# S5's gate inputs in places of their own, head norms summed by column quarters, meta products as whole tiles

## The chip, the core and the metric

One core of a Trainium2 chip runs the whole kernel. TensorE (PE) multiplies, VectorE (DVE) and ScalarE (ACT) work on tiles in the on-chip memory SBUF and read products out of PSUM, GpSimd (POOL) does a few side jobs, SyncE (SP) issues the loads. All engines run beside each other; each works its own queue in order and waits on semaphores. The metric is the device time of one execution in microseconds (us), as a median over runs.

## The reference

One layer of a hybrid encoder over 16 meta tokens and 256 tokens, width 2048, all in float32.

```python
xn = rmsnorm(h, norm_mix); q, f, i, g, u = split(xn @ w_in)      # 5 x 1024 columns
# HGRN2, 8 heads of 128: chunkwise gated recurrence
f = lb + (1 - lb) * sigmoid(f); k = (1 - lb) * sigmoid(-f_logit); q = silu(q)
S_t = diag(f_t) S_{t-1} + k_t v_t^T;  o_t = S_t^T q_t
o = o * rsqrt(mean(o * o over the head) + EPS) * gain * silu(g)   # head norm
# S5, 64 groups of 16 channels, complex diagonal state of 64
y = Re(C x_t) + d * u;  y = gelu(y)
y = y * sigmoid(y @ w_glu + b_glu);  y = rmsnorm(y)               # the gate (GLU)
h = h + concat(o, y) @ w_out
h = h + conv_ffn(rmsnorm(h))                                      # 2048 -> 2 x 5632 -> 2048
out = rmsnorm(h[16:])
```

## The kernel before

Everything is kept channel-major: 128 channels on the partitions, tokens along the columns (272 with the meta tokens, 258 where only the last two of them are needed). Each large product is made as three matmuls in a fast float32 form: weights are split into a high part `whi` (ACT, L163) and the rest `wlo` (DVE, L85), activations likewise into `xh`/`xl`, `gh`/`gl`, `mh`/`ml`; `mm3` (L187 to L189) runs high x high, low x high, high x low into a PSUM tile `acc`. Weights come in 1 MB pieces; `whi` and `wlo` have three buffers each, a piece takes two, and three `acc` tiles rotate.

The mixer runs in the order `u0 h0 u1 h1 u2 h2 u3 h3 g0 .. g3`. A `u` chunk feeds two S5 tiles: projection `bu` (L602, 64-row matmuls), a scan on DVE with ACT and POOL (ending in `xo`, the state), the output products `yps` (L616 and L621, 32-column matmuls), and then the GELU in five steps on DVE and ACT: `ysb` (scale and add), `gq` squared (ACT), `gq` (DVE), sigmoid (ACT), `ysb` (product). An `h` chunk pair makes two HGRN2 heads: the scores `dps`, `lps`, `xps`; then the meta tokens' part, `mps` = `km` x `qm` (L761, 16 meta tokens as 16 output columns), copied to `sm`, and the output `ops`, whose first matmul `vm` x `sm` (L766) contracts over those 16 rows; three more (L767 to L769) follow. `oT` holds the heads' outputs, `gs` the output gates.

Behind the mixer: `gh`/`gl` are made from all eight `ysb` tiles, in one tile of the pool `tl`, which is opened where the pool of S5's working tiles (`s5w`) is closed, in the same memory. The GLU's four products with `w_glu` read them (`acc<-gh`); each result gates `ysb` (`sgl`) and its square is added into `ssum`, summed over channels by `s5s` (L847). The head norm: `sq` squares a head, `hps` (L857) sums it over channels into row h of an 8-row PSUM tile by a weight matrix of 8 columns; `rsqrt` makes the scale in some 13 steps on DVE (`rhv`, `rht`, `rhy`); `hr2` keeps it as high part and rest in 40 rows; `bps` (L868) spreads one head's row over 128 partitions by a 40-row matmul, one at a time in PSUM; then `oT` is scaled and split into `mh`/`ml`. `w_out` is applied in two halves, the first over the HGRN2 heads, the second over S5. The gated MLP follows.

The order on each engine is not that of the code: a scheduler lays the instructions out by a simulated timeline, within priorities (`pri`) and the dependencies of the tiles, and a tile's place in memory makes dependencies too. So an edit of a few lines moves rows all over the mixer stage.

Of the kernel before, what the change touches and what calls it, by code (L numbers as in the profile page):

```python
# [73 lines left out]
def hymba_kernel(ctx: ExitStack, tc: tile.TileContext, x, meta, lb_logits, norm_mix, w_in, hg_norm,  # L74
# [9 lines left out]
    def tt(dst, a, b, op, eng=dve):  # L84
        eng.tensor_tensor(out=dst, in0=a, in1=b, op=op)  # L85
# [572 lines left out]
    def hg_i(accs):  # L658
        iv = hgp.tile([128, 2, T], F32, tag="iv", name="iv")
        for m in range(2):  # L660
            act.copy(out=iv[:, m], in_=accs[m])
# [4 lines left out]
        v = hgp.tile([128, 4, 128], F32, tag="v", name="v")
        act.copy(out=v, in_=tp)
        tp = ptp.tile([128, 4, 128], F32, tag="tp", name="vtp")
        for m in range(2):
            pe.transpose(tp[0:NM, m], iv[:, m, 0:NM], ident)  # L670
        vm = hgp.tile([NM, 2, 128], F32, tag="vm", name="vm")
        act.copy(out=vm, in_=tp[0:NM, 0:2])
        return v, vm

    def hg_g(h0, accs):
        sg = hgp.tile([128, 2, NQ], F32, tag="sg", name="sg")
# [1 line left out]
            fact(sg[:, m], accs[m], AF.Sigmoid)  # L678
            stt(gs[:, h0 + m], accs[m], vcol[:, V_HG + h0 + m:V_HG + h0 + m + 1], sg[:, m], MUL, MUL)

    def hg_group(h0, f, k, q, v, vm):
        SP = hgp.tile([128, 2, T], F32, tag="SP", name="SP")
        pool.memset(SP, 1.0)

# [53 lines left out]
            widen(h)  # L738
        return S, SP

    def hg_cross(h0, f, f15, k, q, v, vm, S, SP):
        kx = hgp.tile([128, 2, 128], F32, tag="qh", name="kx", bufs=3)
        tt(kx, k[:, :, NM:NM + 128], SP[:, :, NM:NM + 128], MUL)
        km = hgp.tile([128, 2, NM], F32, tag="km", name="km")
        tt(km, k[:, :, 0:NM], SP[:, :, 0:NM], MUL)
# [12 lines left out]
        sm = hgp.tile([NM, 2, NQ], F32, tag="iv", name="sm")  # L758
        for m in range(2):
            ps = psc.tile([128, NQ], F32, tag="sc", name="mps")  # L760
            pe.matmul(ps[0:NM], km[:, m], qm[:, m], start=True, stop=True)  # L761
            act.copy(out=sm[:, m, 1:NQ], in_=ps[0:NM, 1:NQ])
            ts(sm[:, m, 0:1], ps[0:NM, 0:1], misc[0:NM, 17:18], MUL)
        for m in range(2):
            ps = psc.tile([128, NQ], F32, tag="sc", name="ops")
            pe.matmul(ps, vm[:, m], sm[:, m], start=True, stop=False)  # L766
# [1 line left out]
            pe.matmul(ps[:, 130:NQ], v[:, 2 * m], sx[:, m], start=False, stop=False)
            pe.matmul(ps[:, 130:NQ], v[:, 2 * m + 1], S[:, 2 * m + 1], start=False, stop=True)  # L769
# [45 lines left out]
    tlp = tls.enter_context(tc.tile_pool(name="tl", bufs=1))  # L815


    gh = tlp.tile([128, 8, 2 * NQ], F32R, name="gh")
    gl = gh[:, :, NQ:2 * NQ]
    gh = gh[:, :, 0:NQ]  # L820

    def sp_view(a):
        return a.rearrange("p (s k) -> p s k", s=2)

    for j in range(8):
        yv = ysb[:, j, :, K0:TH]
        act.copy(out=sp_view(gh[:, j]), in_=yv)
# [22 lines left out]
    mh = xnp.tile([128, KD, T], F32R, tag="xh", name="mh")  # L850
    ml = xnp.tile([128, KD, T], F32R, tag="xl", name="ml")
    with pri(-2):
        hps = psc.tile([8, NQ], F32, tag="sc", name="hps")
        for h in range(NH):
            sq = hgp.tile([128, NQ], F32, tag="qh", name="sq", bufs=3)
            fact(sq, oT[:, h], AF.Square)
            pe.matmul(hps, onehot[:, 7 - h:15 - h], sq, start=(h == 0), stop=(h == NH - 1))  # L857
# [4 lines left out]
        tt(hr2[32:40], hrs, hr2[0:8].bitcast(F32), SUB)
        hsel = hgp.tile([40, NH], F32R, tag="f15", name="hsel")
        dve.tensor_copy(out=hsel, in_=misc[0:40, 18:26])
        for h in range(NH):
# [2 lines left out]
            pe.matmul(bp, hsel[:, h:h + 1].to_broadcast([40, 128]), hr2, start=True, stop=True)  # L868
# [192 lines left out]
```

## Time and profile before

| | us |
|---|---|
| median of 3 runs | 1241.25 (1241.08 to 1242.11) |
| the profiled execution | 1245.4, of which span 1243.6 |
| PE busy | 1220.0 |
| DVE busy | 878.6 |
| ACT busy | 605.9 |
| mean granted PE clock | 0.991 |

The span runs from the first to the last instruction. In rows of the order of time, the first number is the start in us from the span's beginning, the second the length; "x2" merges records of one kind, and an fp32 matmul leaves two records. Ends of matmuls are modelled and they overlap, so what a matmul costs is read from start to start. In brackets stands the idle time of the engine ahead of the row and who ended it.

### The profile page before, as it was taken

To read this page: it belongs to the slowest core of one execution; us is meant where nothing else is said; L and a number is where in the kernel's file an instruction comes from. 1 tells how busy PE (TensorE), PEld (TensorE's weight loads), DVE (VectorE), ACT (ScalarE), POOL (GpSimd) and SP (SyncE) were. 2 spreads that over 40 slices of the span, in tenths; PEclk is the share of its full clock that TensorE was granted. 3 is DMA by queue.
4 is the path that set the end of the run, shared out by engine and by line. 5 is a ranking of instruction groups with operands and counts; after the bars stand their busy time and mean duration, and the time that the engine had idled before them with its cause. 6 is when DMAs were issued, how large, how long until landed. Compare 5 with 4: busy or idle time off the path is not lost.

```text
span 1243.6 us, 22643 instructions
## 1 busy us (share of the span) xinstructions
PE 1220.0 (98%) x9235; PEld 1146.4 (92%) x9235; DVE 878.6 (71%) x1535; ACT 605.9 (49%) x1054; POOL 91.1 (7%) x116
## 2 busy tenths in 40 slices
PE   7999999999999999999999999999999999999997
PEld 6999998989979999999999999999999988888886
DVE  7899999999977877765656656656656644545554
ACT  6756566675645455433433433434333434444454
POOL 5221211322100000000000000000000000000000
PEclk8999999999999999999999999999999999999999
DMA  8454443334335555565555656555565645555552
GB/s 241 147 149 131 143 142 106 113 109 144 127 102 169 171 178 196 170 195 179 183 190 176 197 171 194 179 184 190 174 199 170 230 165 184 200 201 184 191 208 97
DMA packets 176295, 210.73 MB, mean 169 GB/s; under 512 B 14772, under 2 KB 168879, under 8 KB 170415
## 3 DMA queue, kind: packets, MB, share of 16 engines
q1 hardware_dynamic: 175871, 209.20, 51.8%
q8 instruction: 72, 1.18, 0.4%
q14 instruction: 32, 0.26, 0.1%
q0 software_dynamic: 320, 0.09, 0.0%
HBM read 206.05 MB, written 2.10 MB: 167 GB/s over the span
## 4 chain that ended last, share of the span: by engine, by line
PE 95%; DVE 3%; DMA 1%; issue 0%; ACT 0%; SPq 0%; DVEq 0%; ACTq 0%
PE acc L189 10%; PE acc L188 10%; PE acc L187 9%; PE ua L188 7%; PE ua L187 7%; PE ga L187 7%; PE ua L189 7%; PE ga L189 7%; PE ga L188 7%; PE d L984 6%; PE d L982 6%; PE d L983 6%; PE bu L602 1%; PE lps L731 1%; DVE wlo L85 1%; DVE xn L94 1%
## 5 line engine op out<-in xcount | busy, mean ns | idle before, releaser
L85 DVE TENSOR_TENSOR wlo<-raw,whi 128x1024 fp32r<-128x1024 f32 (+1 forms) x376 | 461.2, 1227 | 305.1 <-ACT whi L163 255.6
L163 ACT CAST whi<-raw 128x1024 fp32r<-128x1024 f32 (+1 forms) x382 | 397.8, 1042 | 517.2 <-PE ga L188 158.2
L187 PE MATMUL ga<-fh,whi 128*128 128x258 f32 x704 | 199.0, 283 | 0.5 <-DVE a L85 0.5
L189 PE MATMUL ga<-fh,wlo 128*128 128x258 f32 x704 | 198.5, 282 | 0.0
L188 PE MATMUL ua<-fl,whi 128*128 128x256 f32 x704 | 198.4, 282 | 0.0
L188 PE MATMUL ga<-fl,whi 128*128 128x258 f32 x704 | 198.1, 281 | 0.0
L189 PE MATMUL ua<-fh,wlo 128*128 128x256 f32 x704 | 197.9, 281 | 0.0
L187 PE MATMUL ua<-fh,whi 128*128 128x256 f32 x704 | 197.9, 281 | 0.0
L188 PE MATMUL acc<-xl,whi 128*128 128x272 f32 (+1 forms) x640 | 186.9, 293 | 2.3 <-DVE xl L85 2.3
L189 PE MATMUL acc<-xh,wlo 128*128 128x272 f32 (+1 forms) x640 | 184.3, 293 | 3.8 <-DVE wlo L85 3.8
L187 PE MATMUL acc<-xh,whi 128*128 128x272 f32 (+1 forms) x640 | 185.9, 294 | 0.0
L187 PEld LDWEIGHTS ga<-fh,whi 128*128 128x128 f32 x704 | 133.0, 189 | 0.7 <-DVE a L85 0.7
L188 PEld LDWEIGHTS ga<-fl,whi 128*128 128x128 f32 x704 | 133.5, 190 | 0.0
L187 PEld LDWEIGHTS ua<-fh,whi 128*128 128x128 f32 x704 | 133.1, 189 | 0.0
L189 PEld LDWEIGHTS ua<-fh,wlo 128*128 128x128 f32 x704 | 132.9, 189 | 0.0
L188 PEld LDWEIGHTS ua<-fl,whi 128*128 128x128 f32 x704 | 132.8, 189 | 0.0
L189 PEld LDWEIGHTS ga<-fh,wlo 128*128 128x128 f32 x704 | 132.6, 188 | 0.0
L982 PE MATMUL d<-whi,ah 128*128 128x512 f32 x328 | 127.7, 389 | 0.0
L188 PEld LDWEIGHTS acc<-xl,whi 128*128 128x128 f32 x640 | 121.8, 190 | 6.4 <-DVE xl L85 3.2
L983 PE MATMUL d<-whi,al 128*128 128x512 f32 x328 | 127.6, 389 | 0.0
L189 PEld LDWEIGHTS acc<-xh,wlo 128*128 128x128 f32 x640 | 120.9, 191 | 6.7 <-DVE wlo L85 4.3
L187 PEld LDWEIGHTS acc<-xh,whi 128*128 128x128 f32 x640 | 121.1, 190 | 3.3 <-issue 1.7
(381 smaller groups left out, 1840.3 us busy)
## 6 DMA issues: line engine op xcount, KB each, us to landing
raw<-in_w_ffn_gate SPq DMA_DIRECT2D x44, 1024.0 KB, 5.1
raw<-in_w_ffn_up SPq DMA_DIRECT2D x44, 1024.0 KB, 5.1
raw<-in_w_ffn_down SPq DMA_DIRECT2D x44, 1024.0 KB, 4.8
raw<-in_w_in SPq DMA_DIRECT2D x39, 1024.0 KB, 5.2
raw<-in_w_out SPq DMA_DIRECT2D x16, 1024.0 KB, 5.4
raw<-in_w_glu SPq DMA_DIRECT2D x4, 1024.0 KB, 5.2
x<-in_x SPq DMA_DIRECT2D x4, 512.0 KB, 5.9
out<-ob SPq DMA_DIRECT2D x8, 256.0 KB, 2.8
```

Of the source, the lines that this page charges most:

```text
L85: eng.tensor_tensor(out=dst, in0=a, in1=b, op=op)
L94: dve.scalar_tensor_tensor(out=dst, in0=a, scalar=s, in1=b, op0=op0, op1=op1, **kw)
L163: act.copy(out=hi[:, c], in_=raw[:, hf, c])
L187: pe.matmul(accs[m], lh, xh[:, n0:n1], start=first, stop=False)
L188: pe.matmul(accs[m], lh, xl[:, n0:n1], start=False, stop=False)
L189: pe.matmul(accs[m], ll, xh[:, n0:n1], start=False, stop=end)
L602: return pe.matmul(bus[i][:, ri], bt[h, 2 * ri + q0 // 2], R[h, q0 // 2], start=True, stop=True)
L731: pe.matmul(ps[:, i], kt[:, i], qf[:, 64 * i:64 * (i + 1)], start=True, stop=True)
L982: pe.matmul(dps[t][n], ah[:, tk], hi, start=False, stop=False, skip_group_check=True)
L983: pe.matmul(dps[t][n], al[:, tk], hi, start=False, stop=False, skip_group_check=True)
L984: pe.matmul(dps[t][n], ah[:, tk], lo, start=False, stop=end, skip_group_check=True)
```

## The change

- `gh`/`gl` get one tile for each of the eight S5 tiles: three in the S5 pool, which is open from the start, three in places of the HGRN2 pool that held `f`, `k` and `q` (tags `PP`, `k`, `q`), two in `tl`.
- `km` and `vm` become whole tiles of 128 columns or rows, cleared once by POOL; `mps` gives 128 rows, of which 112 are zero, and `ops` contracts over 128 rows.
- A head's sum goes into one of four 32-column quarters of a 128-row PSUM tile: heads 2q and 2q+1 into quarter q, on alternate rows. The sums are issued in the order 0, 2, 4, 6, 1, 3, 5, 7. The scale is made on all 128 rows; rows 0 and 1 of a quarter keep the high part, rows 2 and 3 the rest (two DVE steps with column masks, `ht` and `hr`), and `bps` contracts over 128 rows, with two PSUM buffers (`bu`) instead of one.
- The constants `misc` grow from 26 to 69 columns.

```diff
-    misc = np.zeros((128, 26), np.float32)
+    misc = np.zeros((128, 69), np.float32)
...
-    misc[:, 18:26] = (s[:, None] % 32 == np.arange(NH)) & (s[:, None] < 64)
+    misc[:, 18:26] = (s[:, None] // 32 == hd // 2) & (s[:, None] % 2 == hd % 2) & (s[:, None] % 32 < 4)
+    misc[:, 26] = (s % 32 < 2) * 1.0 - ((s % 32 >= 2) & (s % 32 < 4))
+    misc[:, 27] = (s % 32 >= 2) & (s % 32 < 4)
+    misc[:, [29, 31]] = 1.0
...
     ysb = s5p.tile([128, 8, 2, TH], F32, name="ysb")
+    ghs = [s5p.tile([128, 2 * NQ], F32R, name=f"gh{i}") for i in range(3)]
...
+    km = hgp.tile([128, 2, 128], F32, name="km")
+    vm = hgp.tile([128, 2, 128], F32, name="vm")
+    for k in kts + [S, km, vm]:
         pool.memset(k, 0.0)
...
-        vm = hgp.tile([NM, 2, 128], F32, tag="vm", name="vm")
-        act.copy(out=vm, in_=tp[0:NM, 0:2])
+        act.copy(out=vm[0:NM], in_=tp[0:NM, 0:2])
...
-        sm = hgp.tile([NM, 2, NQ], F32, tag="iv", name="sm")
+        sm = hgp.tile([128, 2, NQ], F32, tag="iv", name="sm")
         for m in range(2):
             ps = psc.tile([128, NQ], F32, tag="sc", name="mps")
-            pe.matmul(ps[0:NM], km[:, m], qm[:, m], start=True, stop=True)
+            pe.matmul(ps, km[:, m], qm[:, m], start=True, stop=True)
...
-    gh = tlp.tile([128, 8, 2 * NQ], F32R, name="gh")
+    ghs += [hgp.tile([128, 2 * NQ], F32R, tag=t, name="gh" + t) for t in ("PP", "k", "q")]
+    ghs += [tlp.tile([128, 2 * NQ], F32R, name=f"gh{i}") for i in (6, 7)]
+    gh, gl = [z[:, 0:NQ] for z in ghs], [z[:, NQ:2 * NQ] for z in ghs]
...
-        hps = psc.tile([8, NQ], F32, tag="sc", name="hps")
-        for h in range(NH):
+        hps = psc.tile([128, NQ], F32, tag="sc", name="hps")
+        for h in (0, 2, 4, 6, 1, 3, 5, 7):
             sq = hgp.tile([128, NQ], F32, tag="qh", name="sq", bufs=3)
             fact(sq, oT[:, h], AF.Square)
-            pe.matmul(hps, onehot[:, 7 - h:15 - h], sq, start=(h == 0), stop=(h == NH - 1))
-        hrs = rsqrt(hgp, hps, [8, NQ], 1.0 / 128, "rh", tags=("iv", "qm", "v"))
-        hr2 = hgp.tile([40, NQ], F32R, tag="SP", name="hr2")
-        pool.memset(hr2.bitcast(F32), 0.0)
-        act.copy(out=hr2[0:8], in_=hrs)
-        tt(hr2[32:40], hrs, hr2[0:8].bitcast(F32), SUB)
+            pr = slice(16 * h - 16 * (h % 2), 16 * h - 16 * (h % 2) + 32)
+            pe.matmul(hps[pr], misc[:, 29 - h % 2:61 - h % 2], sq, start=(h % 2 == 0), stop=(h % 2 == 1),
+                      skip_group_check=True)
+        hrs = rsqrt(hgp, hps, [128, NQ], 1.0 / 128, "rh", tags=("iv", "qm", "v"))
+        hr = hgp.tile([128, NQ], F32R, tag="SP", name="hr")
+        ht = hgp.tile([128, NQ], F32, tag="iv", name="ht")
+        act.copy(out=hr, in_=hrs)
+        ts(ht, hr.bitcast(F32), misc[:, 26:27], MUL)
+        stt(hr, hrs, misc[:, 27:28], ht, MUL, ADD)
...
-            bp = psc.tile([128, NQ], F32, tag="sc", name="bps")
-            pe.matmul(bp, hsel[:, h:h + 1].to_broadcast([40, 128]), hr2, start=True, stop=True)
+            bp = pbu.tile([128, NQ], F32, tag="bu", name="bps")
+            pe.matmul(bp, hsel[:, h:h + 1].to_broadcast([128, 128]), hr, start=True, stop=True)
```

What the scheduler makes of it is seen at the two places below. Line numbers of the new code are higher: `mm3` is L191 to L193 there, `yps` L621 and L626, `bps` L879.

PE around the start of the GLU, before. The last S5 tile's output products (`yps`) stand among the head sums, then 33 plain matmuls of the last `g` chunk, then the GLU:

```order
L616 MATMUL yps<-xo,cp_570 32x136 x6
L621 MATMUL yps<-xo,cp_570 32x135 x6
L857 MATMUL hps<-sq,misc 8x258
L621 MATMUL yps<-xo,cp_570 32x135
L857 MATMUL hps<-sq,misc 8x258
L621 MATMUL yps<-xo,cp_570 32x135
L187 MATMUL acc<-xh,whi 128x258
...
L189 MATMUL acc<-xh,wlo 128x258
L187 MATMUL acc<-gh,whi 128x258 x3
L188 MATMUL acc<-gh,whi 128x258
```

All S5 tiles are done on PE before the GLU begins. The same engine and place after the change (`gh_589` is the first of the eight tiles, `ghq` the sixth, `gh_4902` the seventh):

```order
L193 MATMUL acc<-xh,wlo 128x258
L191 MATMUL acc<-gh_589,whi 128x258
...
L193 MATMUL acc<-ghq,wlo 128x258
L621 MATMUL yps<-xo,cp_570 32x136 x8
L626 MATMUL yps<-xo,cp_570 32x135 x8
L879 MATMUL bps<-hr,hsel 128x258 x2
L191 MATMUL acc<-gh_4902,whi 128x258 x3
L192 MATMUL acc<-gh_4902,whi 128x258
```

The GLU now starts with 54 matmuls (six of the eight tiles, into three `acc`) ahead of the last S5 tile's `yps`; two `bps` and the last two `gh` tiles come behind it.

DVE at the end of the last S5 scan, before. Its last step is `xo`; the head scale (`rhv`) and the GELU (`ysb<-ysb,vcol,yps`) follow:

```order
L85 TENSOR_TENSOR P<-W,m 128x544
L85 TENSOR_TENSOR wlo<-raw,whi 128x1024
L85 TENSOR_TENSOR xo<-P 128x272
L85 TENSOR_TENSOR oT<-oT,gs 128x258 x3
L85 TENSOR_TENSOR wlo<-raw,whi 128x1024
L91 TENSOR_SCALAR rhv<-hps 8x258
L94 SCALAR_TENSOR_TENSOR ysb<-ysb,vcol,yps 128x272
```

And after:

```order
L90 TENSOR_TENSOR wlo<-raw,whi 128x1024
L90 TENSOR_TENSOR xo<-P 128x272
L90 TENSOR_TENSOR rht<-rhy 128x258
L99 SCALAR_TENSOR_TENSOR rht<-rhv,rht 128x258
L99 SCALAR_TENSOR_TENSOR rhy<-rht,rhy 128x258
L90 TENSOR_TENSOR rht<-rhy 128x258
L99 SCALAR_TENSOR_TENSOR ysb<-ysb,vcol,yps 128x272
L99 SCALAR_TENSOR_TENSOR rht<-rhv,rht 128x258
L99 SCALAR_TENSOR_TENSOR rhy<-rht,rhy 128x258
L99 SCALAR_TENSOR_TENSOR gq<-gq,ysb 128x258
L94 TENSOR_SCALAR ht<-hr,misc 128x258
L90 TENSOR_TENSOR ysb<-ysb,gq 128x2x129
```

More stands ahead of the last `xo` than before: four more `wlo`, six of the `gl` splits, five more products of `oT` with `gs`, two more `gs` and the first six steps of the head scale. The last steps of the head scale are between `xo` and the GELU, and `hr` (next after the last row shown) behind it.

More of the change, by code (lines that the diff above doesn't have):

```diff
@@ L68, in constants @@
     misc[:, 17] = (s != NM - 1)
-    misc[:, 18:26] = (s[:, None] % 32 == np.arange(NH)) & (s[:, None] < 64)
+    hd = np.arange(NH)
+    misc[:, 18:26] = (s[:, None] // 32 == hd // 2) & (s[:, None] % 2 == hd % 2) & (s[:, None] % 32 < 4)
+    misc[:, 26] = (s % 32 < 2) * 1.0 - ((s % 32 >= 2) & (s % 32 < 4))
+    misc[:, 27] = (s % 32 >= 2) & (s % 32 < 4)
+    misc[:, [29, 31]] = 1.0
     return ident, masks.reshape(128, -1), misc
@@ L116, in hymba_kernel @@
     masks = const.tile([128, 5, 64], F32, name="masks")
-    misc = const.tile([128, 26], F32, name="misc")
+    misc = const.tile([128, 69], F32, name="misc")
     ones = const.tile([128, 128], F32, name="ones")
-    onehot = misc[:, 0:15]
     def rsqrt(p, src, shape, scale, nm, eps=EPS, tags=None):
@@ L635, in hymba_kernel @@
     S = hgp.tile([128, 4, 128], F32, name="S")
-    for k in kts + [S]:
+    km = hgp.tile([128, 2, 128], F32, name="km")
+    vm = hgp.tile([128, 2, 128], F32, name="vm")
+    for k in kts + [S, km, vm]:
         pool.memset(k, 0.0)
@@ L670, in hg_i @@
             pe.transpose(tp[0:NM, m], iv[:, m, 0:NM], ident)
-        vm = hgp.tile([NM, 2, 128], F32, tag="vm", name="vm")
-        act.copy(out=vm, in_=tp[0:NM, 0:2])
-        return v, vm
+        act.copy(out=vm[0:NM], in_=tp[0:NM, 0:2])
+        return v
     def hg_g(h0, accs):
@@ L679, in hg_g, with hg_group @@
             stt(gs[:, h0 + m], accs[m], vcol[:, V_HG + h0 + m:V_HG + h0 + m + 1], sg[:, m], MUL, MUL)
-    def hg_group(h0, f, k, q, v, vm):
+    def hg_group(h0, f, k, q, v):
         SP = hgp.tile([128, 2, T], F32, tag="SP", name="SP")
@@ L739, in hg_group, with hg_cross @@
         return S, SP
-    def hg_cross(h0, f, f15, k, q, v, vm, S, SP):
+    def hg_cross(h0, f, f15, k, q, v, S, SP):
         kx = hgp.tile([128, 2, 128], F32, tag="qh", name="kx", bufs=3)
         tt(kx, k[:, :, NM:NM + 128], SP[:, :, NM:NM + 128], MUL)
-        km = hgp.tile([128, 2, NM], F32, tag="km", name="km")
-        tt(km, k[:, :, 0:NM], SP[:, :, 0:NM], MUL)
+        tt(km[:, :, 0:NM], k[:, :, 0:NM], SP[:, :, 0:NM], MUL)
         qm = hgp.tile([128, 2, NQ], F32, tag="qm", name="qm")
@@ L757, in hg_cross @@
         act.copy(out=sx, in_=ps)
-        sm = hgp.tile([NM, 2, NQ], F32, tag="iv", name="sm")
+        sm = hgp.tile([128, 2, NQ], F32, tag="iv", name="sm")
         for m in range(2):
             ps = psc.tile([128, NQ], F32, tag="sc", name="mps")
-            pe.matmul(ps[0:NM], km[:, m], qm[:, m], start=True, stop=True)
-            act.copy(out=sm[:, m, 1:NQ], in_=ps[0:NM, 1:NQ])
-            ts(sm[:, m, 0:1], ps[0:NM, 0:1], misc[0:NM, 17:18], MUL)
+            pe.matmul(ps, km[:, m], qm[:, m], start=True, stop=True)
+            act.copy(out=sm[:, m, 1:NQ], in_=ps[:, 1:NQ])
+            ts(sm[:, m, 0:1], ps[:, 0:1], misc[:, 17:18], MUL)
         for m in range(2):
@@ L799, in do_h @@
         with pri(-3):
-            v, vm = hg_i(accs)
+            v = hg_i(accs)
         with pri(-2):
-            S, SP = hg_group(2 * g, f, k, q, v, vm)
-            hg_cross(2 * g, f, f15, k, q, v, vm, S, SP)
+            S, SP = hg_group(2 * g, f, k, q, v)
+            hg_cross(2 * g, f, f15, k, q, v, S, SP)
     def do_g(c):
@@ L815, in hymba_kernel @@
     tlp = tls.enter_context(tc.tile_pool(name="tl", bufs=1))
-    gh = tlp.tile([128, 8, 2 * NQ], F32R, name="gh")
-    gl = gh[:, :, NQ:2 * NQ]
-    gh = gh[:, :, 0:NQ]
+    ghs += [hgp.tile([128, 2 * NQ], F32R, tag=t, name="gh" + t) for t in ("PP", "k", "q")]
+    ghs += [tlp.tile([128, 2 * NQ], F32R, name=f"gh{i}") for i in (6, 7)]
+    gh, gl = [z[:, 0:NQ] for z in ghs], [z[:, NQ:2 * NQ] for z in ghs]
     def sp_view(a):
@@ L826, in hymba_kernel @@
         yv = ysb[:, j, :, K0:TH]
-        act.copy(out=sp_view(gh[:, j]), in_=yv)
-        tt(sp_view(gl[:, j]), yv, sp_view(gh[:, j]).bitcast(F32), SUB)
+        act.copy(out=sp_view(gh[j]), in_=yv)
+        tt(sp_view(gl[j]), yv, sp_view(gh[j]).bitcast(F32), SUB)
     ssum = tlp.tile([128, NQ], F32, name="ssum")
@@ L832, in hymba_kernel @@
         accs = [pmm.tile([128, NQ], F32, tag="mm", name="acc") for _ in range(2)]
-        mm3(accs, u, lambda kt: (gh[:, kt], gl[:, kt]), 0, NQ)
+        mm3(accs, u, lambda kt: (gh[kt], gl[kt]), 0, NQ)
         with pri(-3):
@@ L852, in hymba_kernel @@
     with pri(-2):
-        hps = psc.tile([8, NQ], F32, tag="sc", name="hps")
-        for h in range(NH):
+        hps = psc.tile([128, NQ], F32, tag="sc", name="hps")
+        for h in (0, 2, 4, 6, 1, 3, 5, 7):
             sq = hgp.tile([128, NQ], F32, tag="qh", name="sq", bufs=3)
             fact(sq, oT[:, h], AF.Square)
-            pe.matmul(hps, onehot[:, 7 - h:15 - h], sq, start=(h == 0), stop=(h == NH - 1))
-        hrs = rsqrt(hgp, hps, [8, NQ], 1.0 / 128, "rh", tags=("iv", "qm", "v"))
-        hr2 = hgp.tile([40, NQ], F32R, tag="SP", name="hr2")
-        pool.memset(hr2.bitcast(F32), 0.0)
-        act.copy(out=hr2[0:8], in_=hrs)
-        tt(hr2[32:40], hrs, hr2[0:8].bitcast(F32), SUB)
-        hsel = hgp.tile([40, NH], F32R, tag="f15", name="hsel")
-        dve.tensor_copy(out=hsel, in_=misc[0:40, 18:26])
+            pr = slice(16 * h - 16 * (h % 2), 16 * h - 16 * (h % 2) + 32)
[7 more added lines that the diff above has]
+        stt(hr, hrs, misc[:, 27:28], ht, MUL, ADD)
+        hsel = hgp.tile([128, NH], F32R, tag="f15", name="hsel")
+        dve.tensor_copy(out=hsel, in_=misc[:, 18:26])
         for h in range(NH):
             tt(oT[:, h], oT[:, h], gs[:, h], MUL)
-            bp = psc.tile([128, NQ], F32, tag="sc", name="bps")
-            pe.matmul(bp, hsel[:, h:h + 1].to_broadcast([40, 128]), hr2, start=True, stop=True)
+            bp = pbu.tile([128, NQ], F32, tag="bu", name="bps")
+            pe.matmul(bp, hsel[:, h:h + 1].to_broadcast([128, 128]), hr, start=True, stop=True)
             tt(oT[:, h], oT[:, h], bp, MUL)
```

## The prediction

> **What bounds the kernel now.** I read the page's busy times first, then the waits of TensorE (PE), then its busy time and clock by stretch, then the order of time around the places of the change.
>
> ```profile
> PE 1220.0 (98%) x9235; PEld 1146.4 (92%) x9235; DVE 878.6 (71%) x1535; ACT 605.9 (49%) x1054; POOL 91.1 (7%) x116
> ```
> ```profile
> PE acc L189 <- DVE wlo L85: 3.8, 2, 2.1
> ...
> PE acc L187 <- ACT gh L827: 1.6, 1, 1.6
> ```
> ```profile
> 60.00:340.00 280.00, 276.20 (x2415) 254.19 (x2415) 268.05 (x552) 175.25 (x464) 65.84 (x76) 0.99 0.42 129
> ...
> 75.00:79.00 4.00, 3.69 (x18) 3.69 (x19) 4.00 (x9) 1.38 (x4) 1.93 (x5) 0.57 0.00 0
> 199.00:203.00 4.00, 2.30 (x19) 2.08 (x18) 4.00 (x3) 1.30 (x2) 0.00 (x0) 1.00 0.00 0
> 361.00:365.00 4.00, 1.23 (x6) 0.62 (x5) 3.95 (x10) 3.78 (x10) 0.00 (x0) 1.00 0.81 257
> 365.00:369.00 4.00, 4.00 (x22) 4.00 (x22) 3.90 (x12) 0.00 (x0) 0.00 (x0) 0.57 0.02 5
> ```
> The second block is who PE waited for (total, times, longest); the third gives, for a stretch of time, its length, busy us of PE, weight load, DVE, ACT and POOL, then the granted clock. PE is the bound: 98%. But in the mixer stage (60 to 340 us) VectorE (DVE) is busy for 268.05 of 280 us, so there two engines are near full, and PE time saved there shows only as far as DVE keeps up. Around the start of the GLU (361 to 365 us) PE works 1.23 of 4 us and stands 2.8, 1.6 of it for the first `gh`; right after it the clock is 0.57 over 4 us: 0.43 x 4 = 1.7 us more. The same follows the wait of 2.1 us at 73 us (0.57 from 75 on); the wait of 1.7 us at 201 us left the clock at 1.00.
>
> **The change: what PE saves.** A matmul's modelled length says little, so I take start to start.
>
> ```profile
> 340.69 0.28 PE L188 MATMUL acc<-xl,whi 128*128 128x258 f32 x1
> 340.81 0.28 PE L189 MATMUL acc<-xh,wlo 128*128 128x258 f32 x1
> 341.02 0.70 PE L766 MATMUL ops<-sm,vm 16*128 16x258 f32 x2
> ...
> 341.97 0.39 PE L768 MATMUL ops<-sx,v 128*128 128x128 f32 x2
> 342.19 0.39 PE L769 MATMUL ops<-S,v 128*128 128x128 f32 x2
> ...
> 342.54 0.29 PE L188 MATMUL acc<-xl,whi 128*128 128x258 f32 x1
> ```
> ```profile
> 401.26 0.60 PE L847 MATMUL s5s<-ssum,ones 128*128 128x258 f32 x2
> ...
> 401.94 0.28 PE L188 MATMUL acc<-ml,whi 128*128 128x258 f32 x1
> ```
> ```profile
> 334.08 0.28 PE L187 MATMUL acc<-xh,whi 128*128 128x258 f32 x1
> 334.29 0.61 PE L761 MATMUL mps<-qm,km 128*16 128x258 f32 x2
> ...
> 335.06 0.40 PE L612 MATMUL yps<-ysb,k 128*128 128x136 f32 x2
> ```
> ```profile
> 372.74 0.29 PE L188 MATMUL acc<-gh,whi 128*128 128x258 f32 x1
> 372.95 0.38 PE L868 MATMUL bps<-hr,hsel 40*128 40x258 f32 x1
> ...
> 373.49 0.28 PE L187 MATMUL acc<-gh,whi 128*128 128x258 f32 x1
> ```
> A plain matmul of 258 columns takes 0.12 (340.69 to 340.81). A full-height fp32 one (s5s, two records) with two plain ones behind it takes 0.68, so 0.44 alone. That is the price of the new forms.
>
> - `ops` (16 rows, 8 of them): 341.02 to 342.54 is 1.52 us for it, three pairs behind it at 0.22 and one plain one; as a full tile 0.44 + 0.66 + 0.12 = 1.22. Entering it costs 0.21 where a plain step is 0.12. Saving 0.39 x 8 = 3.1 us.
> - `mps` (16 columns, 8): 334.29 to 335.06 is 0.77 against 0.56, and 0.09 at the entry: 0.30 x 8 = 2.4. Some will stand beside `bu`, whose 64-row shape breaks the stream anyway: I take 2.0.
> - `bps` (40 rows, 8): 372.95 to 373.49 is 0.54 against 0.24, and 0.09: 0.39 x 8 = 3.1 us.
> - `hps` (8 columns, 8 of them). In the new order three head sums of different quarters stand together, and two more.
>
> ```profile
> 349.76 1.47 PE L857 MATMUL hps<-sq,misc 128*8 128x258 f32 x6
> ```
> ```profile
> 297.10 0.67 PE L616 MATMUL yps<-xo,cp 128*32 128x136 f32 x16
> 297.59 0.64 PE L621 MATMUL yps<-xo,cp 128*32 128x135 f32 x16
> ```
> Today three (six records) take some 1.4 us, one after the other. The S5 outputs use 32-column quarters already: eight matmuls in four quarters, two rounds, take 0.49, so a round of 136 columns takes 0.25 and one of 258 some 0.47 (an estimate). Three together save 0.9, two together 0.4: 1.3; I take 1.2.
>
> Small edits: the constants' load grows from 26 to 69 columns and POOL clears two more tiles at the start, both far off PE's path (POOL 7% busy); operations over 128 rows instead of 8 cost per column, as the rows of 8x258 and 128x258 below show (0.41 and 0.41 to 0.42); one DVE operation more in the head scale. Nothing for these, with up to 0.5 us as bound.
>
> **What moves around the GLU.** The new places let six of the eight `gh`/`gl` pairs be made early, so the GLU's first wait (1.6) goes. But in the new order 54 GLU matmuls now stand ahead of the last S5 tile's `yps`, and behind it PE has only two `bps` and then `gh6`, both of which hang on that tile or on the head scale. So the wait is moved, not gone. When does the last `xo` come?
>
> ```profile
> 350.17 0.43 DVE L85 TENSOR_TENSOR xo<-P 128x272 f32<-128x272 f32 x1
> ```
> ```profile
> 357.44 0.48 DVE L94 SCALAR_TENSOR_TENSOR ysb<-ysb,vcol,yps 128x272 f32<-128x272 f32 x1
> ...
> 358.40 0.43 DVE L94 SCALAR_TENSOR_TENSOR gq<-gq,ysb 128x258 f32<-128x258 f32 x1
> 358.75 0.41 DVE L85 TENSOR_TENSOR rht<-rhy 8x258 f32<-8x258 f32 x1
> 359.19 0.42 DVE L94 SCALAR_TENSOR_TENSOR rht<-rhv,rht 8x258 f32<-8x258 f32 x1
> 359.54 1.21 DVE L85 TENSOR_TENSOR wlo<-raw,whi 128x1024 fp32r<-128x1024 f32 x1
> 360.67 0.41 DVE L85 TENSOR_TENSOR ysb<-ysb,gq 128x258 f32<-128x258 f32 x1
> ...
> 363.34 0.42 DVE L85 TENSOR_TENSOR oT<-oT,gs 128x258 f32<-128x258 f32 x1
> 363.67 0.48 DVE L94 SCALAR_TENSOR_TENSOR gs<-acc,vcol,sg 128x258 f32<-128x258 f32 x1
> 364.07 0.41 DVE L94 SCALAR_TENSOR_TENSOR rht<-rhv,rht 8x258 f32<-8x258 f32 x1
> 364.40 0.75 DVE L85 TENSOR_TENSOR gh<-ysb,gh 128x258 fp32r<-128x258 f32 x2
> ```
> ```profile
> 359.22 0.41 ACT L82 ACTIVATE gq<-gq 128x258 f32<-128x258 f32 x1
> ```
> Today it ends at 350.6. DVE's new order has 23 operations more ahead of it: 4 `wlo` at 1.15 (start to start), 6 `gl` at 0.35, 5 `oT` products at 0.33, 2 `gs` at 0.40, 6 steps of the head scale at 0.36: 4.6 + 2.1 + 1.7 + 0.8 + 2.2 = 11.4 us. With DVE 96% busy I take its idle time as unchanged: 350.6 + 11.4 = 362.0.
>
> PE would be there earlier. Its work ahead of the GLU ends at 361.2 (362.80 less the 1.60 of idle in the row below); without `yps` (from 297.10 to the end of 297.59 + 0.64, 1.1) and with 54 x 0.12 = 6.5 that is 366.6, less 3.1 + 2.0 + 1.2 of shapes 360.3, and less the waits on `wlo` at 73 and 201 us (3.8, and 1.7 of clock), if they go, 354.8. So `xo` sets it: 362.0, plus 1.1 of `yps`, plus the chain that PE then waits for: `ysb` 0.48, two head-scale steps 0.42 + 0.41, `gq` 0.43, the sigmoid on ACT 0.41, `ysb` 0.41, the last head-scale step 0.48, together 3.0. At 366.1 PE goes on with `bps`. A wait of 3.0 us is longer than the one of 2.1 that dropped the clock, so I leave the 1.7 in.
>
> ```profile
> 362.80 0.51 PE L187 MATMUL acc<-gh,whi 128*128 128x258 f32 x2 [1.60 <-ACT gh L827]
> ```
> ```profile
> 440.40 0.28 PE L187 MATMUL acc<-mh,whi 128*128 128x258 f32 x1
> ```
> From the GLU's start to the second half of the output projection (its first matmul at 440.40) PE takes 77.6 us today. Of that the 54 matmuls (6.5) are done by then, the rest of the standing at its start goes (2.8 - 1.6 = 1.2), `bps` saves 3.1: 66.8. So this point comes at 366.1 + 66.8 = 432.9, 7.5 us earlier. From there on both orders are the same.
>
> What is late next: behind the waiting `bps` stand the last 18 GLU matmuls of that block, and DVE's products with `bps` and ACT's `mh` wait for them; the sum over S5 (`s5s`) comes 92 matmuls later than today. The S5 scale then has the 226 matmuls up to the projection's second half, 27 us at 0.12, for 28 operations of some 0.41 on DVE, six sums into `xT` at the same and five `wlo` at 1.15: about 20 us. I cost that at nothing; if that cover were gone, PE would stand at the second half's first matmul.
>
> The sum: 1243.6 - 7.5 = 1236.1 us of span. The profiled execution took 1245.4 us, 1.8 around its span and 4.15 above the median of the runs, so I take the 7.5 from the median: 1233.7 us. A difference under 0.2% (2.5 us) is about what a measurement of this kernel cannot tell from none.
>
> **Rivals.**
> *DVE keeps up, PE alone bounds.* Much of DVE's idle time waits on PE itself:
> ```profile
> DVE wlo L85 <- ACT whi L163: 7.7, 13, 2.4
> ```
> (60 to 351 us.) If PE is faster these shrink, `xo` comes with PE at about 357.5 (the middle of 354.8 and 360.3), and the sum is 4.5 us lower: 1229 us. Against it: in the new order `wlo` stands earlier among S5's rows, which makes DVE wait for it more often.
>
> *The clock stays up after the moved wait.* The Trainium skill, "TensorE: Matmul & The Clock Gate", section "Why this matters for your kernels", has the PE fall back to half clock only after gaps over about 3 us, one window of idle. By that the moved wait might pass at full clock, 1.7 us less: 1232.0 us. The trace speaks against it: 2.1 us were enough at 73 us, 1.7 were not at 201.
>
> *The gain is used up, or worse, by `wlo` ahead of S5.* DVE runs in order. The last `wlo` before `xo` needs a cast that needs one of three weight buffers, free only when PE has done 30 matmuls of the GLU; each such wait holds S5's steps behind it. If DVE's waits on `whi` grow from 7.7 to 15 us, `xo` comes at 369.5 and nothing is left: 1241 us. Past 372 us the kernel is slower by over 0.2%: at 18 us of waits, 1244 us. For it: DVE has only 12 us of slack in 280. Against it: `wlo` stands earlier in the new queue than today (the 58th is DVE's 582nd instruction today and its 553rd then), so PE has less reason to wait.
>
> **How the numbers follow.** The forecast of DVE setting the last tile (1231 to 1237) has 0.5, the clock that stays up 0.1, PE alone 0.17, the gain used up 0.15, slower 0.08. The first three are faster: 0.77. The range leaves out the slower case and most of the one used up: 1228 to 1239.5.
>
> **What would show it.** Right: records of `ops`, `mps` and `bps` as 128 rows by 128 columns, with a plain step ahead of them of 0.12; no wait on `gh L827` at the GLU's start, but one of about 3 us before `bps` or `gh6`, right after the last `yps`, and a granted clock near 0.57 behind it; `xo` ending near 362 and the projection's second half starting near 433. Wrong: `xo` past 366, new waits of PE on `wlo` between 60 and 340 us, or the steps into `ops` still at 0.21.

## The result, and the profile after

The changed kernel takes 1234.22 us (median; 1234.08 to 1234.66), beside 1241.68 for the kernel before: a ratio of 0.9934, 95% interval 0.9916 to 0.9952, 7.5 us less. Timed again later beside other kernels it took 1233.64 against 1242.14 (0.9925, 0.9912 to 0.9938). The forecast was 1233.7.

The page of the changed kernel, the line of busy times:

```profile
PE 1210.4 (98%) x9235; PEld 1145.0 (93%) x9235; DVE 878.9 (71%) x1536; ACT 607.4 (49%) x1054; POOL 91.3 (7%) x117
```

PE's waits behind 60 us (total, times, longest):

```profile
PE bps L879 <- DVE hr L99: 3.2, 1, 3.2
PE ktp L557 <- ACT bt L553: 1.0, 1, 1.0
```

Two of its stretches (length, busy us of PE, weight load, DVE, ACT, POOL, then the granted clock):

```profile
60.00:340.00 280.00, 278.40 (x2466) 260.18 (x2465) 270.85 (x556) 180.72 (x477) 64.85 (x74) 1.00 0.43 133
365.00:369.00 4.00, 4.00 (x25) 4.00 (x25) 2.63 (x6) 2.88 (x8) 0.00 (x0) 0.65 0.00 0
```

PE is 9.6 us less busy. Both waits on `wlo` and the one on `gh` are gone. A new one of 3.2 us stands ahead of `bps`, and a stretch at half clock follows it. PE's order of time shows the new shapes and the moved wait:

```profile
323.13 0.28 PE L193 MATMUL acc<-xh,wlo 128*128 128x258 f32 x1
323.25 0.60 PE L767 MATMUL mps<-qm,km 128*128 128x258 f32 x2
323.50 0.47 PE L191 MATMUL acc<-xh,whi 128*128 128x258 f32 x1
323.80 0.28 PE L192 MATMUL acc<-xl,whi 128*128 128x258 f32 x1
...
335.27 0.61 PE L865 MATMUL hps<-sq,misc 128*32 128x258 f32 x6
335.81 0.39 PE L193 MATMUL acc<-xh,wlo 128*128 128x258 f32 x1
...
352.08 0.28 PE L191 MATMUL acc<-gh,whi 128*128 128x258 f32 x1
...
359.57 0.64 PE L626 MATMUL yps<-xo,cp 128*32 128x135 f32 x16
363.44 0.48 PE L879 MATMUL bps<-hr,hsel 128*128 128x258 f32 x2 [3.22 <-DVE hr L99]
...
429.29 0.28 PE L191 MATMUL acc<-mh,whi 128*128 128x258 f32 x1
...
475.39 0.28 PE L191 MATMUL ga<-fh,whi 128*128 128x258 f32 x1
```

The step into `mps` is a plain 0.12, and it takes 0.43 alone (323.25 to 323.80 less one plain step). Three head sums (six records) are through in 0.54 (335.27 to 335.81) where three took 1.4. The row at 429.29 is the first matmul of the second half of `w_out`, the last row the first one of the MLP. From that second half to the end of the span all fourteen traces of this case take 803.2 us, so whatever they differ by lies ahead of it.

### The profile page after: what moved, and what is told of

Its sections match the earlier page's. It is cut to its first block, busy times and chain, and to the rows that moved or that the text cites. A ratio compares the mean times of both kernels' runs of the same rounds, so it can differ in the third digit from the quotient of the medians.

```text
span 1232.5 us, 22657 instructions
## 1 busy us (share of the span) xinstructions
PE 1210.4 (98%) x9235; PEld 1145.0 (93%) x9235; DVE 878.9 (71%) x1536; ACT 607.4 (49%) x1054; POOL 91.3 (7%) x117
## 4 chain that ended last, share of the span: by engine, by line
PE 93%; DVE 4%; ACT 2%; issue 1%; DMA 0%; SPq 0%; DVEq 0%; ACTq 0%
PE acc L192 9%; PE acc L191 9%; PE acc L193 9%; PE ua L192 7%; PE ua L191 7%; PE ga L191 7%; PE ua L193 7%; PE ga L193 7%; PE ga L192 7%; PE d L995 6%; PE d L993 6%; PE d L994 6%; PE bu L607 1%; PE lps L738 1%; DVE wlo L90 1%; DVE xn L99 1%
## 5 line engine op out<-in xcount | busy, mean ns | idle before, releaser
L191 PE MATMUL ga<-fh,whi 128*128 128x258 f32 x704 | 199.0, 283 | 0.5 <-DVE a L90 0.5
L193 PE MATMUL ga<-fh,wlo 128*128 128x258 f32 x704 | 198.5, 282 | 0.0
L193 PE MATMUL ua<-fh,wlo 128*128 128x256 f32 x704 | 197.9, 281 | 0.0
L191 PE MATMUL ua<-fh,whi 128*128 128x256 f32 x704 | 197.9, 281 | 0.0
L191 PE MATMUL acc<-xh,whi 128*128 128x272 f32 (+1 forms) x640 | 185.2, 293 | 0.1
L193 PE MATMUL acc<-xh,wlo 128*128 128x272 f32 (+1 forms) x640 | 183.8, 292 | 0.0
L191 PEld LDWEIGHTS ga<-fh,whi 128*128 128x128 f32 x704 | 133.0, 189 | 0.7 <-DVE a L90 0.7
L191 PEld LDWEIGHTS ua<-fh,whi 128*128 128x128 f32 x704 | 133.1, 189 | 0.0
L193 PEld LDWEIGHTS ua<-fh,wlo 128*128 128x128 f32 x704 | 132.9, 189 | 0.0
L193 PEld LDWEIGHTS ga<-fh,wlo 128*128 128x128 f32 x704 | 132.6, 188 | 0.0
L191 PEld LDWEIGHTS acc<-xh,whi 128*128 128x128 f32 x640 | 120.5, 189 | 2.5 <-issue 0.4
L193 PEld LDWEIGHTS acc<-xh,wlo 128*128 128x128 f32 x640 | 120.1, 189 | 2.8 <-issue 1.5
```

Source lines behind the costliest of these rows:

```text
L191: pe.matmul(accs[m], lh, xh[:, n0:n1], start=first, stop=False)
L193: pe.matmul(accs[m], ll, xh[:, n0:n1], start=False, stop=end)
```

## The experiments

**The kernel before, once more.**

> The kernel before, profiled a second time, because its first profiled execution ran 4.15 us above the median of its runs while the trace of the changed kernel starts the second half of the output projection 11.1 us earlier. Theory (the 7.5 us are real, the other 3.6 belong to that one execution): this execution is near 1241.5 us, starts the second half near 437 us, and the wait of PE on the rest of the weights at 73 us or the one at 201 us is shorter or gone. Rival (the waits at 73 and 201 us and the half clock behind the first belong to the kernel's order): both are there again with 2.1 and 1.7 us, the granted clock is 0.57 from 75 us on, and the time is near 1245.

It took 1240.78 us, span 1239.0. PE's waits behind 60 us, and neighbouring stretches around 199 us and around the GLU's start:

```profile
PE acc L189 <- DVE wlo L85: 3.6, 2, 1.8
PE acc L187 <- ACT gh L827: 1.6, 1, 1.6
```

```profile
196.05:199.46 3.41, 1.59 (x14) 1.37 (x12) 3.41 (x3) 1.03 (x2) 0.00 (x0) 1.00 0.00 0
199.46:202.87 3.41, 3.41 (x23) 2.79 (x23) 3.41 (x8) 0.83 (x3) 0.95 (x1) 1.00 0.64 216
356.48:359.89 3.41, 1.81 (x15) 1.60 (x14) 3.36 (x7) 2.31 (x7) 0.00 (x0) 1.00 0.31 82
359.89:363.30 3.41, 2.23 (x15) 1.82 (x16) 3.41 (x10) 1.92 (x7) 0.00 (x0) 1.00 0.64 226
363.30:366.71 3.41, 3.41 (x30) 3.41 (x29) 2.83 (x9) 0.56 (x2) 0.00 (x0) 1.00 0.00 0
```

The waits are all there, so they belong to the order (the rival was right in that), but nothing between 60 and 1230 us ran at half clock, and the time is not the rival's 1245. In the first profiled execution of the same kernel:

```profile
71.70:75.11 3.41, 1.51 (x26) 1.25 (x25) 3.41 (x4) 2.03 (x6) 1.48 (x2) 1.00 0.11 10
75.11:78.52 3.41, 3.21 (x14) 3.21 (x15) 3.41 (x9) 1.38 (x4) 1.82 (x5) 0.50 0.00 0
361.84:365.25 3.41, 1.27 (x6) 0.87 (x7) 3.36 (x8) 3.06 (x10) 0.00 (x0) 1.00 0.97 306
365.25:368.66 3.41, 3.41 (x19) 3.41 (x18) 3.34 (x10) 0.00 (x0) 0.00 (x0) 0.50 0.00 1
```

The clock record changes in steps of 3.413 us, and all changes of an execution lie on one grid (75.11 and 365.25 are 85 steps apart). At the GLU's start PE stands for 2.8 us in both executions. In the first, 2.14 of it falls into one step (3.41 less 1.27) and the next step runs at half clock; in the second the grid splits it into 1.6 and 1.2, and the clock stays up. The order of PE is the same in both, so the 4.6 us between the two spans can be followed from matmul to matmul: 1.5 are there by the 101st matmul of the mixer's projections (39.7 against 38.2 us), where the first execution has more half clock; 1.6 come around 75 us, 0.3 of it a longer wait on `wlo`; 1.5 come in the step at 365 us. So a step at half clock cost 1.3 and 1.5 us, not the 1.7 of the prediction, which took half of the time as lost.

**Each part alone.** Three kernels, each the kernel before with one of the three edits of the diff: the places of `gh` and `gl`; `km`, `vm`, `mps` and `ops` as whole tiles; the head norm (`hps`, `hr`, `bps`).

> The kernel before with the places of gh and gl alone changed; products and head norm as before. Theory (PE's shapes carry the gain, the wait at the GLU's start is only moved): the last S5 tile's outputs stand one matmul ahead of the GLU, the first use of the seventh tile 55 matmuls (6.6 us) behind them, longer than the GELU and the cast (about 3 us), so here the wait on gh (1.6 us) and the half clock behind it (1.7 us) go unless xo comes later with DVE's order: between 1238.4 and 1241.7. Rival (the early gh carry most of the gain): 1236 or less. Rival (gl ahead of S5's rows hold up DVE): over 1242, with new waits of PE on xo or yps.

> The kernel before with the meta products alone as whole tiles. Theory (shape prices on PE's path): ops 3.1 us and mps 2.0 us less, 1241.7 - 5.1 = 1236.6; the step into ops is 0.12 and not 0.21, and the last outputs of S5 come some 5 us earlier, since xo (350.6) waits for PE there and not the reverse. Rival (DVE, busy 96% in this stage, sets the pace): DVE's own work is unchanged, PE waits for wlo or xo instead, gain at most 1.5 us: 1240 to 1241.7.

> The kernel before with the head norm alone changed (sums in column quarters, scale on 128 rows, spread over 128 rows with two buffers). Theory (shape prices on PE's path): hps 1.2 and bps 3.1 us less, 1241.7 - 4.3 = 1237.4; but its order puts the last S5 outputs directly ahead of the GLU, with nothing between, so PE waits there for the GELU and the gh cast, about 3.0 us in place of 1.6: 1238.8. Rival (bps and hps stand beside waits, not on the path): no gain, 1241 to 1242.5.

| part alone | us | before | ratio, 95% |
|---|---|---|---|
| `gh`, `gl` | 1238.90 | 1242.28 | 0.9966 (0.9954 to 0.9978) |
| meta products | 1240.55 | 1242.28 | 0.9987 (0.9978 to 0.9996) |
| head norm | 1243.58 | 1242.28 | 1.0004 (0.9991 to 1.0017) |

The three medians add up to 3.8 us less, half of what they give together. The first came as expected; the other two missed.

With the meta products alone 1236.6 had been expected. The GLU starts at 357.63 where the second execution of before has 359.71. Of these 2.1 us the mixer's earlier start made 0.3, and against them stand a step at half clock at 198.78 (some 1.5) and waits on `wlo` that are 0.5 longer: 2.1 - 0.3 + 1.5 + 0.5 = 3.8 us of shapes (an estimate), of 5.1 forecast. They are partly lost again, to the clock: the 1.9 us of standing at 198 us and the 2.5 us in one step at the GLU's start were each followed by a step at half clock.

With the head norm alone 1238.8 had been expected, and the kernel is no faster than before. Its times fall in two groups, 1238.86 to 1240.99 and 1243.09 to 1246.74; the profiled execution is of the lower one, so what makes the upper one is not known. The order puts `yps` straight ahead of the GLU, and the wait forecast at 3.0 is 4.7:

```profile
362.53 0.80 PE L191 MATMUL acc<-gh,whi 128*128 128x258 f32 x2 [4.72 <-ACT gh L831]
```

```profile
361.45:364.86 3.41, 2.33 (x11) 2.33 (x12) 3.38 (x11) 2.79 (x9) 0.00 (x0) 0.50 0.00 0
364.86:368.28 3.42, 3.42 (x17) 3.42 (x17) 1.70 (x5) 0.09 (x1) 0.00 (x0) 0.50 0.00 0
```

Two steps at half clock follow. With `gh` alone PE has one wait left near 73 us and none at the GLU. So the prices of these parts do not add: here a part's shapes show in the time only as far as no wait or half clock takes them back.

**Without the head norm's part.** `gh`/`gl` and meta products together:

> The kernel before with gh/gl places and whole-tile meta products, the head norm as before (8-row sums, 40-row spread). Its order puts the last S5 outputs two matmuls ahead of the GLU and the first use of the seventh gh tile 57 matmuls (6.8 us) behind them. Theory (the parts depend on each other: the meta products' shape savings show in full once nothing waits at the GLU's start; the head norm's 4.3 us of shapes are paid back by the 3.2 us wait before bps and the half clock behind it, 1.7): 1238.9 (gh alone) less some 4.7 = 1234.2, the same as the whole change, no wait over 0.5 us near the GLU. Rival (the parts simply add): 1238.9 - 1.7 (meta alone) = 1237.2, and the head norm gives the remaining 3.

1234.63 us, ratio 0.9934 (0.9917 to 0.9952), the same as the whole change. PE's waits over 0.25 us between 60 us and the MLP are these two:

```profile
PE acc L189 <- DVE wlo L85: 2.1, 1, 2.1
...
PE ops L767 <- DVE sm L89: 0.4, 1, 0.4
```

The theory holds (the parts added up would have been 1237.2): the head norm's part pays for its own wait and clock and adds nothing that these runs can tell.

**The wait filled.** The changed kernel, with work that the result doesn't need behind the last `yps` (`last[0]`); the order is otherwise the same:

```diff
+            if h == 0:
+                with tc.issue_after(last[0].ins):
+                    for _ in range(7):
+                        pe.matmul(bp, ident, oT[:, 7], start=True, stop=True)
             pe.matmul(bp, hsel[:, h:h + 1].to_broadcast([128, 128]), hr, start=True, stop=True)
```

> The changed kernel with seven extra fp32 matmuls (ident times a finished head, into the PSUM tile that the first bps overwrites) directly behind the last yps, 7 x 0.44 = 3.1 us of work where PE waited 3.2 us; the order on all engines is otherwise the same. Theory (the traces so far: the clock is granted in steps of 3.413 us; a step in which PE stood 1.84 us or more was followed by half clock, one with 1.82 us or less was not): no half clock inside the span between 60 and 1200 us, 1.7 us less: 1232.5. Rival (the drop does not come from the standing, but from the work behind it): still one step at half clock, 1234.2. Rival (the extra work delays the spread): bps later by up to 1 us, 1233.5.

> The changed kernel with the seven extra matmuls in the wait before bps, beside the changed kernel itself on the same chip. Theory (clock alone): 1.7 us less than the changed kernel in this call, at most 0.4 of it lost where the extra work ends after the wait. Rival (the first run's 2.7 us less were real in full): 2.5 us or more less. Rival (the first difference was the chip's): under 0.8 us.

> The changed kernel again, timed beside the next two on the same chip. Its first four times were 1234.08 to 1234.66; in its trace the half clock falls three steps of 3.413 us within the first 60 us and once at 364 us. Theory (what varies between executions is where the fixed 3.413 us steps fall against the waits): 1232.5 to 1235.5; one step at half clock behind the wait before bps in the profiled execution. Rival (the wait of 3.2 us depends on the chip or the execution): it is under 2 us this time.

1231.51 us (0.9909, 0.9890 to 0.9928), and beside the changed kernel on the same chip 1231.45 (0.9912, 0.9898 to 0.9927) against 1233.64: 2.2 us less, between the expected 1.7 and the rival's 2.5. The changed kernel's second trace has the wait of 3.2 us again and one step at half clock behind it, as expected. The traces tell the gain more finely than the medians. From the GLU's start to the MLP's first matmul both profiled executions of the changed kernel take 123.31 us, those of the filled kernel 121.99 and 121.97, so 1.3 less. No step behind the filled wait runs at half clock. The rows of the second of these traces, and ten microseconds of it:

```profile
358.07 3.31 PE L883 MATMUL bps<-oT,ident 128*128 128x258 f32 x14
361.27 0.50 PE L884 MATMUL bps<-hr,hsel 128*128 128x258 f32 x2
```

```profile
354.00:364.00 10.00, 9.88 (x90) 8.62 (x89) 9.37 (x23) 3.79 (x9) 0.00 (x0) 1.00 0.46 139
```

**The wait half filled.** Three matmuls in place of seven.

> As the kernel with seven extra matmuls behind the last yps, but with three (3 x 0.47 = 1.4 us by the trace of the seven), so that PE still stands some 1.8 us before the spread. It tells whether the clock falls by the length of standing or by the mere wait. Theory (half clock follows only a 3.413 us step with 1.84 us or more of standing): the spread starts as with seven, no step at half clock behind it in most executions, 1231.5 as with seven. Rival (any wait of over 1 us ahead of dense work drops the clock): one step at half clock, 1.7 more: 1233.

```profile
356.64 0.28 PE L191 MATMUL acc<-gh,whi 128*128 128x258 f32 x1
...
364.44 1.57 PE L883 MATMUL bps<-oT,ident 128*128 128x258 f32 x6
367.66 0.50 PE L884 MATMUL bps<-hr,hsel 128*128 128x258 f32 x2 [1.65 <-DVE hr L99]
...
478.29 0.28 PE L191 MATMUL ga<-fh,whi 128*128 128x258 f32 x1
```

```profile
365.00:369.00 4.00, 2.35 (x16) 1.89 (x15) 3.76 (x12) 1.96 (x6) 0.00 (x0) 1.00 0.62 212
369.00:373.00 4.00, 4.00 (x35) 3.94 (x34) 3.58 (x9) 3.77 (x9) 0.00 (x0) 1.00 0.00 0
```

At the place the theory holds: PE stands 1.65 us and the clock stays at 1.00. From the GLU's start to the MLP it takes 121.65 us, 1.66 less than the changed kernel. Not all of that is the clock: `bps` starts 11.02 us behind the GLU's start (367.66 less 356.64) where the changed kernel has 11.36 (363.44 less 352.08), and from `bps` to the MLP the two take 110.63 and 111.95. So the step at half clock cost 1.3 us. The median, 1234.35 (0.9930, 0.9912 to 0.9947), is above both the 1231.5 expected and the rival's 1233. The times fall in two groups, 1231.45 to 1232.68 and 1236.01 to 1237.24; the profiled execution belongs to the upper one, and there the time went near 80 us and not at this wait (last section). The other two of that group left no trace.

**Less in front of the last `xo`.** `gl` of six tiles on POOL (`tt(sp_view(gl[j]), yv, ..., SUB, pool)`), and in another kernel the last two S5 tiles at a higher priority (`with pri(-1)` around `s5_tile`):

> The changed kernel with the first six gl subtractions on POOL instead of DVE. The order changes with it: 21 rows and two wlo fewer on DVE ahead of the last xo, the last S5 outputs 18 matmuls into the GLU instead of 54, the seventh gh tile first used 36 matmuls (4.3 us) behind them. Theory (DVE's queue ahead of xo, unbroken from 347.6 us on, sets the 3.2 us wait): wait and half clock both go, 1234.2 - 3.2 - 1.7 = 1229.3. Rival (PE sets it through the weight buffers, so xo comes no earlier against PE): the wait is only moved, 1233 to 1235. Rival (POOL's subtractions are late or slow DVE down): new PE waits on gl, over 1235.

> The changed kernel with the last two S5 tiles at a higher priority in the scheduler. The last S5 outputs stand 36 matmuls into the GLU instead of 54, and 18 plain matmuls (2.2 us) stand between them and the seventh gh tile. Theory (an order that gives PE something to do behind the last yps removes the wait): the chain of some 3.4 us is covered but for 1.2 us, too short to drop the clock: 1234.2 - 2.0 - 1.7 = 1230.5. Rival (S5 ahead of the weight splits starves PE): new waits on wlo between 200 and 350 us take it back, 1234 or more.

1234.20 (0.9924, 0.9900 to 0.9948) and 1232.91 (0.9925, 0.9903 to 0.9946), where 1229.3 and 1230.5 had been expected: not told apart from the changed kernel. With `gl` on POOL the wait before `bps` is gone, a wait on `gh` of 0.4 is left and no half clock near it; with the priority 1.7 on `gh` and 1.3 on `wlo` came in its place. But both traces have this one, as has the second trace of the changed kernel:

```profile
PE acc L191 <- ACT whi L167: 3.1, 1, 3.1
```

Taken to equal terms (that wait of 3.1 and a half-clock step behind it, 1.4, left out) the second half of `w_out` starts 387.4 and 388.5 us behind the 101st matmul of the mixer's projections, and 389.9 in the first trace of the changed kernel: an estimate of 2.5 and 1.4 us sooner. Whether the shorter DVE queue alone would give the 4.9 us in the time stays open.

**Only the spread of the head norm.** The kernel without the head norm's part, with `bps` over 128 rows and two buffers:

```diff
-        hr2 = hgp.tile([40, NQ], F32R, tag="SP", name="hr2")
+        hr2 = hgp.tile([128, NQ], F32R, tag="SP", name="hr2")
...
-            bp = psc.tile([128, NQ], F32, tag="sc", name="bps")
-            pe.matmul(bp, hsel[:, h:h + 1].to_broadcast([40, 128]), hr2, start=True, stop=True)
+            bp = pbu.tile([128, NQ], F32, tag="bu", name="bps")
+            pe.matmul(bp, hsel[:, h:h + 1].to_broadcast([128, 128]), hr2, start=True, stop=True)
```

> The kernel without the head norm's change (gh/gl places and meta products only), and of the head norm only the spread changed: hr2 and its selector have 128 rows (88 or more of them zero), bps contracts over 128 rows and has two buffers; sums and scale stay on 8 rows. On PE and DVE its order is that of the kernel without the head norm's change up to the first bps. Theory (bps at 0.44 in place of 0.83 is 0.39 x 8 = 3.1 us on PE's path, and no wait is put in its place): 1234.6 - 3.1 = 1231.5, faster than the whole change by 2.7. Rival (bps stands beside other waits): 1234.6.

1231.95 us (0.9914, 0.9899 to 0.9929), 2.7 less than without it (timed on another chip), 1.7 less than the whole change on the same chip. From the GLU's start to the MLP it takes 118.49 us, where the kernel without it takes 121.72: 3.2 for the forecast 3.1. Inside these 3.2 a new wait on `wlo` costs 1.0 us, and eight steps between plain matmuls, which without it take 0.22 to 0.43 in place of 0.12 around 390 us, are plain again, 1.2 us; the rest is the shapes. (The 0.44 in its expectation is a slip: `bps` leaves one record and stands at a plain step.)

```profile
371.57 0.28 PE L187 MATMUL acc<-gh,whi 128*128 128x258 f32 x1
371.69 0.28 PE L869 MATMUL bps<-hr,hsel 128*128 128x258 f32 x1
371.81 0.28 PE L188 MATMUL acc<-gh,whi 128*128 128x258 f32 x1
```

This kernel and the filled one are the fastest, and equal to each other within what was measured.

## Why the prediction was right, step by step

*The moved wait* came as forecast: 54 GLU matmuls, the last `yps`, then PE waits 3.2 us (3.0 forecast) for the head scale. *The half clock behind it* came too, at 1.3 us and not 1.7; its size did not enter the forecast, since a step at half clock stood behind the GLU's start in the base as well. The rival in which the clock stays up is refuted for this wait: both traces of the changed kernel have the step. The Trainium skill, "TensorE: Matmul & The Clock Gate", section "Why this matters for your kernels", puts the fall at gaps over about 3 us. Here 1.9 us in one step were enough, and 2.8 us across two were not.

*The shapes:* the meta products alone gave some 3.8 of 5.1; `bps` came to the forecast 3.1; three head sums at once gave 0.86 of 0.9. Part of what the meta products lack shows in the changed kernel's trace, where a whole-tile `ops` stands behind a `bu` or behind a plain matmul:

```profile
327.24 0.50 PE L607 MATMUL bu<-R,bt 64*128 64x136 f32 x4
327.67 0.70 PE L772 MATMUL ops<-sm,vm 128*128 128x258 f32 x2
328.21 0.39 PE L773 MATMUL ops<-S,v 128*128 128x128 f32 x2
...
332.14 0.60 PE L772 MATMUL ops<-sm,vm 128*128 128x258 f32 x2
332.57 0.38 PE L773 MATMUL ops<-S,v 128*128 128x128 f32 x2
```

It takes 0.54 in the first place and 0.43 in the second: beside another odd shape the price of the change of shape stays. Taken to equal terms (the mixer's start and one step at half clock out), the second execution of before and the changed kernel differ by (1239.0 - 38.2) - (1232.5 - 39.4 - 1.3) = 9.0 us. PE's waits over 0.25 us between 60 us and the MLP fall from 6.4 to 4.6, so 7.2 are left for the shapes and what goes with them, where 9.4 had been forecast.

*What failed* is the last `xo` at 362.0. It ended at 358.70:

```profile
358.28 0.42 DVE L90 TENSOR_TENSOR xo<-P 128x272 f32<-128x272 f32 x1
```

The stretch from the 101st matmul of the mixer's projections to the end of the last `xo`, in the first and second execution of before and then in the changed kernel (length, then busy us of PE, weight load and DVE):

```profile
39.67:350.60 310.93, 307.13 (x2657) 283.57 (x2656) 295.77 (x648) 195.31 (x503) 72.42 (x88) 0.99 0.42 131
38.19:347.51 309.32, 305.70 (x2657) 282.14 (x2656) 296.19 (x648) 195.31 (x503) 71.21 (x88) 1.00 0.43 132
```

```profile
39.42:358.70 319.28, 317.11 (x2768) 296.81 (x2767) 306.58 (x676) 204.03 (x519) 73.13 (x89) 1.00 0.43 135
```

DVE's work ahead of `xo` grew by 10.8 or 10.4 us, not 11.4. Its idle time is 15.2 and 13.1 us before, 12.7 after (16.2 in the second trace of the changed kernel, which holds the 3.1 us named above). Against the second execution it is unchanged within 0.4, as the forecast had it; the other 2.0 lie between two executions of one kernel. So the step that failed is the base: 350.6, and with it an idle time of DVE that this kernel need not have, was read out of an execution with a step at half clock near 75 us. From the second execution the same working gives 347.5 + 11.4 = 358.9. The rival "DVE keeps up" finds little support: DVE's waits on `whi` in these stretches are 9.1, 7.5 and 9.2 us, so a faster PE did not shorten them. In both traces of the changed kernel `xo` ends 6.6 us behind the GLU's start, wherever that falls.

PE so went on 2.7 us sooner than forecast, and the second half of `w_out` came 11.1 us earlier, not 7.5. That this did not show in the total has the same cause: the profiled execution of before was 4.15 us above its median, and its second half started late, at 440.40. Counted from the 101st matmul, the second half starts 400.73 and 397.58 us later in the two executions of before, 393.23 in the forecast and 389.87 in the changed kernel. The base was 3.15 us late and the forecast 3.36: the two mistakes cancel, and the total was right partly by luck.

## What to carry to other kernels

A wait that is moved is not removed: count the work that stands behind the producer in the new order, and if it is shorter than the chain, the shapes saved elsewhere go into that wait. Take half-clock steps out of a profiled execution before using it as a base: each was worth 1.3 to 1.5 us here, and an execution had none to two of them behind its first 60 us. Where a short wait can't be closed, filling it with matmuls that nobody needs was worth the step.

## What the runs showed of the hardware

*The clock step.* In the fourteen traces of this case, between 60 and 1200 us, every step of 3.413 us at full clock with 1.84 us or more of PE standing was followed by one at half clock (ten steps, the shortest in the kernel with `gh` alone at 71.75 us), and none with 1.6 or less. Of two with 1.82 one was (`gl` on POOL, 81.92 us) and one was not (the second execution of before, 196.05 us). A half-clock step with 0.8 or 1.1 us of standing was followed by a second, none with 0.2 or less. At half clock a plain matmul took 0.21 from start to start in place of 0.12, as here behind the wait in the changed kernel, so the step's loss is less than half of its length:

```profile
364.53 0.42 PE L192 MATMUL acc<-gh,whi 128*128 128x258 f32 x1
364.74 0.42 PE L193 MATMUL acc<-gh,wlo 128*128 128x258 f32 x1
```

*A small POOL operation that took 12 times its length.* POOL makes `bt` and `br` for S5; an operation of ACT that reads `br` stands ahead of a `whi` in ACT's queue. In the first trace of the changed kernel, and then in the second:

```profile
75.11 0.58 POOL L90 TENSOR_TENSOR bt<-br,abr 128x64 f32<-128x64 f32 x1 [12.54 <-DMA br<-in_s_b_re]
```

```profile
74.29 6.82 POOL L90 TENSOR_TENSOR bt<-br,abr 128x64 f32<-128x64 f32 x1 [12.57 <-DMA br<-in_s_b_re]
```

In the second ACT waits 7.0 us for it and PE 3.1 for the `whi` behind. This is the 3.1 us of four of the traces, the half-filled kernel's among them, where two steps at half clock follow it. During the 6.82 us DVE ran one operation with two inputs after the other; POOL's ended beside this one, which has one:

```profile
80.86 0.29 DVE L94 TENSOR_SCALAR pw<-pt 128x32 f32<-128x32 f32 x1
```

The Trainium skill, "SBUF — State Buffer", section "SBUF: two separate sides", has the two engines share a port pair as an exclusive lock, against DVE operations with two SBUF inputs. The rows of the second trace agree with that; in the first, POOL went through beside the same DVE operations, and no run took them away, so the cause is not shown.
